# The sample's final state in a state-space layer: one set of fp32 products on row tiles, and a new order around scan 6

## The chip, the cores and the metric

The kernel runs on one core of a Trainium2 chip. The metric is the device time of one execution in microseconds (us), as a median over runs. TensorE is called PE (its weight loads PEld), VectorE DVE, ScalarE ACT, GpSimd POOL, and SyncE, which here issues most transfers, SP.

## What is computed

One step of a two-layer decoder trunk: a Mamba-2 (SSD) layer and a pooling layer, each with modulation, norm, gate and residual. Two inputs go through it: a prompt of 1024 new tokens, and a sample of 8 sequences with 8 tokens each and their stored states. The part that the change touches is the final state of the sample in the SSD layer. Each of 32 heads has a state of 64 x 128; four heads form a group, and eight groups are worked on one after another ("scan 0" to "scan 7").

```
def step(h, inp):            # per chunk; the sample has one chunk of 8 tokens
    s, d = inp
    return d[..., None, None] * h + s, h
chunk_states = einsum('bctgn,bctgr,bctgrp->bcgrpn', B, decay_end, xdt)
h_final, h_prev = lax.scan(step, h0, (chunk_states, chunk_decay))
```

For each of the 8 sequences the new state is thus the old one, decayed, plus a product of B and of the weighted x over that sequence's 8 tokens. The 64 sample tokens lie on partitions (twice, to fill 128), so this is a product whose sum runs over 8 of 64 rows.

## The kernel before

Everything in the SSD layer is paced by hand. `ssd_layer` runs eight calls of `scan`, and each has four steps p = 0 to 3 over 256 tokens. Between the pieces of a scan `units(fill, n)` puts in units of other work that PE can do at any time: 24 matmuls `mm` of the input projection of the next group (three matmuls for each of 8 slices of `hn`, split in high and low parts), and from scan 6's end the output product `op`. The table `PACE[g][p]` gives how many units go in at three places of a step. Each engine runs its instructions in the order of the code as a scheduler has merged them, so an instruction that waits holds up all behind it.

In step p, `scan_front(p + 1)` transposes x and B (`tr`, eight matmuls), `scan_state(p)` makes the chunk's states on PE (`S<-xd,Bt`) in the one PSUM bank with the tag "S", which DVE then adds to the running state (`h<-hd,S`), and `scan_y(p)` makes `y` in one of two banks of tag "y", which `scan_evac` empties on DVE (line 588, `xbc<-xbc,vec,y`). At steps p = 2 and 3 the sample is worked: `sample_front` makes Ms, the decays `ea`, the weighted x `xd` and the transposed B in `Bs`; `sample_prep` on p = 3 decays the old state h0 on POOL (line 682) and makes masked copies of x, one for each sequence (`st`, `xm`, ACT). The products themselves, `sample_state`, come during the next scan: half 0 (four sequences) at p = 0, behind y and am, and half 1 at p = 1. Each is four matmuls of 128 x 512 in fp32r, B split in a high and a low part, with one bank of tag "y" and the bank "S", an add on DVE (line 704) and a store on SP. In scan 7 both halves come at p = 0, the first with two "y" banks at its very start.

`ADA` lists the steps (g, p) at which a piece of the modulation vectors is computed. The first half of one is 16 matmuls (`am<-wr,scp`) in a "y" bank, copied by ACT as `mp` (line 266), the second half, after a unit, `am<-kc,mp`, which DVE reads as shf, scl or gat. `gate_norm` (`ms`) and `gate_scale` finish the scan before. The projection's weights come as `wr`, split by ACT and DVE into `wh` and `wl` (lines 152, 153); its result goes through a convolution of four steps: one on ACT, three on DVE (lines 356 to 361, `raw`, `xbc`). Around scan 6 and 7 the rows of gated y come back from memory (`row<-gyd`) and are combined in blocks on DVE (`b`, `bs`).

Of the kernel before, what the change touches and what calls it, by code (L numbers as in the profile page):

```python
# [7 lines left out]
F32 = mybir.dt.float32  # L8
F32R = mybir.dt.float32r
# [5 lines left out]
P = 128  # L15
# [20 lines left out]
         1: ((0, 0, 1), (1, 1, 1)), 4: ((0, 0, 1), (1, 0, 1)), 7: ((0, 0, 1),)}  # L36
LAST_USE = {4: 0, 7: 1}
LEAD = 3
PACE = (((1, 1, 1), (0, 1, 2), (0, 1, 2), (0, 1, 2)),) * 6 + (((1, 1, 1), (0, 1, 2), (0, 3, 5), (0, 1, 1)), ((1, 1, 1), (0, 1, 1), (0, 1, 1), (0, 1, 1)))
ADA = tuple((g, p) for g in range(7) for p in ((0, 1, 2) if g == 0 else (0, 2, 3) if g == 1 else (0, 2)))  # L40
NSLOT_A = 30
NSLOT_B = 7
NSLOT_E = 4
# [63 lines left out]
class Build:  # L107
# [298 lines left out]
    def proj_group(self, G):  # L406

        nc = self.nc
        for ii in range(4):
            w = self.stream_next()  # L410
            raw = self.proj_begin(G, ii)
            if (G["g"], ii) == (7, 3):

                ps = [self.mm_tile() for _ in CH]
                for k in range(8):
                    for c in range(3):
                        self.mm1(ps[c], w, k, self.hn[k], CH[c], k == 0, k == 7)
                    self.slots.free(*self.hn[k])
                    if k < 7:
                        yield  # L420
                for c in range(3):
                    self.proj_evict(G, ii, raw, ps[c], c)
                yield
                return
            for c, (a, n) in enumerate(CH):
                ps = self.mm_tile()
                self.mm3(ps, w, self.hn, CH[c])
                self.proj_evict(G, ii, raw, ps, c)
                yield
# [206 lines left out]
    def sample_front(self, s):  # L636

        nc, gp = self.nc, self.gs
        tok, col = slice(NP, TOK), 4 * s.g
        pt = self.pp.tile([P, 512], F32, tag="tr", bufs=2, name=self.name("tr"))  # L640
        for i, t in enumerate((s.xs[0], s.xs[1], s.B)):
            self.dup(pt[:, 128 * i:128 * i + 128], t[:, tok], self.ident)
        self.dup(pt[:, 384:448], s.B[:, tok], s.C[:, tok])
        A = gp.tile([P, 1024], F32, tag="M", bufs=2, name=self.name("Ms"))
        M, ea = (A[:, 256 * i:256 * i + 256].rearrange("p (r t) -> p r t", r=4) for i in range(2))
        xd = A[:, 512:1024].rearrange("p (i r q) -> p i r q", i=2, r=4)
        nc.vector.tensor_tensor(out=xd, in0=pt[:, 0:256].rearrange("p (r q) -> p r q", r=4).unsqueeze(1).to_broadcast([P, 2, 4, 64]),
                                in1=self.tks[:, :, col:col + 4].unsqueeze(3).to_broadcast([P, 2, 4, 64]), op=ALU.mult)
        Bt = gp.tile([P, 2, 128], F32R, tag="Bs", bufs=1, name=self.name("Bs"))
        nc.scalar.activation(Bt[:, 0], pt[:, 256:384], AF.Copy)  # L650
        nc.vector.tensor_tensor(out=Bt[:, 1], in0=pt[:, 256:384], in1=Bt[:, 0].bitcast(F32), op=ALU.subtract)
        cb = gp.tile([P, 256], F32, tag="cb", bufs=1, name=self.name("cb"))[:, :64]
        nc.vector.tensor_tensor(out=cb, in0=pt[:, 384:448], in1=self.kc[:, K_SMASK:K_SMASK + 64], op=ALU.mult)
        self.tab(nc.scalar.activation(ea, s.acs, AF.Exp))
        for r in range(4):
            nc.scalar.activation(M[:, r], s.acs[:, r], AF.Relu, bias=self.tka[2][:, col + r:col + r + 1], scale=-1.0)
        self.tab(nc.scalar.activation(M, M, AF.Exp, scale=-1.0))
        nc.vector.tensor_tensor(out=M, in0=M, in1=cb.unsqueeze(1).to_broadcast([P, 4, 64]), op=ALU.mult)
        s.sample = (M, ea, xd, Bt)
        self.slots.free(s.B, s.C)  # L660
# [12 lines left out]
        for q in range(2):  # L673
            self.scan_evac(s, q, py[:, q], slice(NP, TOK))

    def sample_prep(self, s):

        nc = self.nc
        _, ea, xd, _ = s.sample
        for i in range(2):  # L680
            h0 = s.hsl[i][:, :1024].rearrange("p (b r q) -> p b r q", b=4, r=4)
            nc.gpsimd.tensor_tensor(out=h0, in0=h0, in1=ea[:, :, 32 * i + 7:32 * i + 32:8].rearrange("p r b -> p b r").unsqueeze(3).to_broadcast([P, 4, 4, 64]), op=ALU.mult)
        xv = xd[:, 1].rearrange("p r q -> p (r q)")
        st = self.gs.tile([P, 256], F32R, tag="st", bufs=1, name=self.name("st"))
        nc.scalar.activation(st, xv, AF.Copy)
        nc.vector.tensor_tensor(out=st[64:], in0=xv[64:], in1=st[64:].bitcast(F32), op=ALU.subtract)
        s.xm = []
        for half in range(2):
            t = self.slots.get("xm", F32R)
            for i in range(4):  # L690
                b = 4 * half + i
                nc.scalar.activation(t[:, 256 * i:256 * i + 256], st.bitcast(F32), AF.Copy, scale=self.kc[:, K_SEQ + b:K_SEQ + b + 1])
            s.xm.append(t)

    def sample_state(self, s, half, tags=("y", "S")):

        Bt = s.sample[3]
        for i in range(2):
            S = self.pp.tile([P, 512], F32, tag=tags[i], bufs={"y": 2, "S": 1}[tags[i]], name=self.name("S"))
            xm = s.xm[half][:, 512 * i:512 * i + 512]  # L700
            self.te.matmul(S, Bt[:, 0], xm, start=True, stop=False)
            self.te.matmul(S, Bt[:, 1], xm, start=False, stop=True)
            d = s.hsl[half][:, 512 * i:512 * i + 512]
            self.nc.vector.tensor_tensor(out=d, in0=d, in1=S, op=ALU.add)
        self.nc.sync.dma_start(self.io["hsT"][s.g][:, 1024 * half:1024 * half + 1024], s.hsl[half][:, :1024])
        self.slots.free(s.hsl[half], s.xm[half])

    def gate_load(self, s):

# [739 lines left out]
    def fills(self):  # L1449

        for g in range(1, 7):
            yield from self.proj_fill(g)
        pr = self.proj_fill(7)
        yield from itertools.islice(pr, 9)
        self.op_begin(0)
        self.optags = ("mm",)
        self.rows = [None] * 16
        blk = self.block_steps(2, self.rows, False, 3, self.load_row)
        for j, _ in enumerate(pr):
            if j == 4:  # L1460
                for _ in range(2):
                    self.ow_fetch()
                self.ow_add()
            next(blk, None)
            yield
        self.ow_split()
        self.ow_fetch()
        self.ow_add()
        for _ in blk:
            pass  # L1470
        self.x = [None] * 8
        yield from self.out_fill()

# [5 lines left out]
    def ssd_layer(self):  # L1479

        self.pinned = True
        fill = self.fills()
        self.tc.keep_in_program_order(self.tab(self.nc.scalar.preload_act_table_set("natural_log_exp_and_others")))
        s = self.scans[0]
        self.scan_ac(s, 0)
        next(fill)
        self.scan_front(s, 0)
        self.scan_decay(s, 0)
        self.scan_ac(s, 1)
        for _ in range(LEAD - 1):  # L1490
            next(fill)
        for s in self.scans:
            self.scan(s, fill)
        self.units(fill, 2)
        self.gate_norm(s)
        self.sample_state(s, 0)
        self.units(fill, 2)
        self.sample_state(s, 1)
        self.gate_scale(s)
        self.pinned = False  # L1500
        self.fill = fill
# [11 lines left out]
    def scan(self, s, fill):  # L1513
# [2 lines left out]
        last, after = self.scans[g - 1] if g else None, self.scans[g + 1] if g < 7 else None  # L1516
        for p in range(4):
            a, b, c = PACE[g][p]
            if p == 0 and g == 7:
                self.sample_state(last, 0, ("y", "y"))  # L1520
            self.units(fill, a)
            if p < 3:
                self.scan_front(s, p + 1)
# [11 lines left out]
            if p == 2:  # L1535
                self.sample_front(s)
                self.sample_inter(s)
            if last and p == 1:
                self.gate_norm(last)
            ada = self.ada(g, p)  # L1540
            next(ada, None)
            if last and p == 0:
                self.sample_state(last, int(g == 7))
            if p == 2:
                self.gate_load(s)
                if g == 6:
# [1 line left out]
            elif p == 3:  # L1548
                if g < 6:
                    self.silu_burst(after.T)  # L1550
                self.sample_prep(s)
                if g == 7:
                    self.gate_rows(s)
            self.units(fill, min(c, 1))
            for _ in ada:
                pass
            if p == 1:
                if last and g < 7:
                    self.sample_state(last, 1)
                self.sample_load(s)  # L1560
            if last and p == 2:
                self.gate_scale(last)
            self.units(fill, c - min(c, 1))
            if p == 3 and after:
                if g == 6:
# [216 lines left out]
def _layout(inputs):  # L1782
# [59 lines left out]
    sc[[0, 128]] = 0  # L1842
    sc[256::8] = 0
    kc[:, K_SCAN:K_SCAN + 320] = sc
    kc[:, K_SEQ:K_SEQ + 8] = (np.arange(128)[:, None] % 64 // 8 == np.arange(8)[None, :])
    for gi, wd in enumerate(WINDOWS):
        for t in range(wd - 1):
            kc[:, K_CNT + 15 * gi + t] = wd / (t + 1.0)
# [34 lines left out]
```

## Time and profile before

| | before |
| --- | --- |
| median of 3 runs | 1656.43 us (1654.96 to 1656.57) |
| profiled execution | 1655.05 us |
| its span | 1653.1 us, mean granted clock 0.980 |
| PE busy | 1592.7 us, 96% |
| DVE, ACT, POOL busy | 76%, 50%, 29% |

The profile shows one execution. Busy time leaves out register, branch, semaphore and DMA-issuing instructions. An instruction's row gives its start, its duration, its line (a helper's, for matmuls L98), tile names out<-in, and in brackets the idle time ahead of it with what released it. The granted clock is 1.00 at 2.4 GHz and 0.50 at 1.2 GHz. The scans lie between about 283 and 900 us of the span.

### The profile page before, as it was taken

To read this page: it belongs to the slowest core of one execution; us is meant where nothing else is said; L and a number is where in the kernel's file an instruction comes from. 1 tells how busy PE (TensorE), PEld (TensorE's weight loads), DVE (VectorE), ACT (ScalarE), POOL (GpSimd) and SP (SyncE) were. 2 spreads that over 40 slices of the span, in tenths; PEclk is the share of its full clock that TensorE was granted. 3 is DMA by queue.
4 is the path that set the end of the run, shared out by engine and by line. 5 is a ranking of instruction groups with operands and counts; after the bars stand their busy time and mean duration, and the time that the engine had idled before them with its cause. 6 is when DMAs were issued, how large, how long until landed. Compare 5 with 4: busy or idle time off the path is not lost.

```text
span 1653.1 us, 30937 instructions
## 1 busy us (share of the span) xinstructions
PE 1592.7 (96%) x12335; PEld 1534.6 (93%) x12335; DVE 1248.2 (76%) x1984; ACT 831.8 (50%) x1485; POOL 475.4 (29%) x516
## 2 busy tenths in 40 slices
PE   8999999999999999998889999999999999999997
PEld 6899999999898989897878999999999999999997
DVE  6874476767777787767798878978889867577876
ACT  6653336666666757575754356633322234333364
POOL 0233441303121212213120122456666640000231
PEclk9999999999999999999889999999999999999999
DMA  8422226435454453637688883133323469566673
GB/s 342 160 98 95 87 73 226 145 111 172 156 167 150 144 194 113 212 117 266 175 287 313 219 196 124 57 110 113 112 90 110 135 204 380 153 169 179 162 155 117
DMA packets 103935, 272.31 MB, mean 165 GB/s; under 512 B 17744, under 2 KB 41712, under 8 KB 103792
## 3 DMA queue, kind: packets, MB, share of 16 engines
q1 hardware_dynamic: 95728, 244.91, 43.3%
q0 software_dynamic: 8064, 25.43, 8.8%
q8 instruction: 97, 1.59, 0.4%
q14 instruction: 46, 0.38, 0.1%
HBM read 208.99 MB, written 56.86 MB: 161 GB/s over the span
## 4 chain that ended last, share of the span: by engine, by line
PE 76%; DVE 10%; ACT 5%; issue 4%; DMA 4%; POOL 2%; SPq 0%; DVEq 0%; POOLq 0%; ACTq 0%
PE st L98 28%; PE mm L98 21%; PE op L98 14%; PE pl L98 3%; PE y L98 2%; DVE raw L358 2%; PE S L98 2%; PE am L98 1%; DMA x<-xT 1%; PE ms L98 1%; DVE M L562 1%; PE tr L98 1%; DVE xbc L359 1%; DMA rs<-rsd 1%; PE tr L101 1%
## 5 line engine op out<-in xcount | busy, mean ns | idle before, releaser
L98 PE MATMUL op<-b,w 128*128 128x272 f32 x2688 | 355.6, 294 | 15.9 <-ACT w L1141 5.4
L98 PEld LDWEIGHTS op<-b,w 128*128 128x128 f32 x2688 | 348.4, 193 | 22.4 <-DVE b L1082 7.0
L98 PE MATMUL st<-hh,w 128*128 128x272 f32 x1408 | 273.8, 289 | 0.0
L98 PE MATMUL mm<-hh,wh 128*128 128x364 f32 x720 | 247.9, 344 | 0.0
L98 PE MATMUL mm<-hl,wh 128*128 128x364 f32 x720 | 239.2, 332 | 0.0
L98 PE MATMUL mm<-hh,wl 128*128 128x364 f32 x720 | 239.0, 332 | 0.0
L98 PEld LDWEIGHTS st<-hh,w 128*128 128x128 f32 x1408 | 224.6, 189 | 0.3 <-issue 0.3
L98 PE MATMUL st<-t,w 128*128 128x272 f32 x1584 | 205.3, 288 | 0.0
L98 PE MATMUL st<-hl,w 128*128 128x272 f32 x704 | 203.5, 289 | 0.0
L98 PEld LDWEIGHTS st<-t,w 128*128 128x128 f32 x1584 | 201.0, 188 | 0.0
L98 PEld LDWEIGHTS mm<-hh,wh 128*128 128x128 f32 x720 | 137.8, 191 | 9.0 <-issue 6.7
L187 ACT ACTIVATE w<-wr 128x512 fp32r<-128x512 f32 x88 | 55.5, 631 | 176.0 <-PE st L98 145.4
L98 PEld LDWEIGHTS mm<-hl,wh 128*128 128x128 f32 x720 | 137.7, 191 | 1.3
L98 PEld LDWEIGHTS mm<-hh,wl 128*128 128x128 f32 x720 | 137.6, 191 | 0.0
L98 PEld LDWEIGHTS st<-hl,w 128*128 128x128 f32 x704 | 132.6, 188 | 0.0
L580 POOL TENSOR_TENSOR hd<-h,cd 128x256 f32<-128x256 f32 x56 | 64.3, 1148 | 135.5 <-DVE h L581 77.4
L1161 DVE SCALAR_TENSOR_TENSOR x<-op,gat,x 128x272 f32<-128x272 f32 (+1 forms) x160 | 72.9, 480 | 38.9 <-PE op L98 32.6
L1141 ACT ACTIVATE w<-wr 128x1024 fp32r<-128x1024 f32 x56 | 59.1, 1055 | 80.3 <-PE op L98 55.8
L363 POOL COPY ncv<-raw 128x3 f32<-128x3 f32 x32 | 8.9, 277 | 312.9 <-ACT raw L434 302.3
L558 ACT ACTIVATE M<-acb,tka 128x128 f32<-128x128 f32 x256 | 82.8, 389 | 25.3 <-PE y L98 15.8
L358 DVE SCALAR_TENSOR_TENSOR raw<-raw,vec,raw 128x1112 f32<-128x1112 f32 x64 | 89.0, 1390 | 6.1 <-ACT raw L356 5.8
L939 DVE TENSOR_TENSOR u<-st,u 128x272 f32<-128x272 f32 (+1 forms) x158 | 61.4, 409 | 39.7 <-PE st L98 37.7
(271 smaller groups left out, 3288.2 us busy)
## 6 DMA issues: line engine op xcount, KB each, us to landing
wr<-win SPq DMA_DIRECT2D x48, 512.0 KB, 3.5
acb<-acd SPq DMA_DIRECT2D x32, 512.0 KB, 5.8
wr<-pin SPq DMA_DIRECT2D x32, 512.0 KB, 3.6
wr<-wout SPq DMA_DIRECT2D x28, 512.0 KB, 6.4
wr<-pout SPq DMA_DIRECT2D x28, 512.0 KB, 4.7
row<-gyd SPq DMA_DIRECT2D x22, 544.0 KB, 7.0
wr<-wout POOLq DMA_DIRECT2D x20, 512.0 KB, 7.9
wr<-pout POOLq DMA_DIRECT2D x20, 512.0 KB, 5.9
```

Of the source, the lines that this page charges most:

```text
L98: return self.pin(self.build.nc.tensor.matmul(*a, **k))
L101: return self.pin(self.build.nc.tensor.transpose(*a, **k))
L187: self.nc.scalar.activation(hi, src, AF.Copy)
L358: nc.vector.scalar_tensor_tensor(out=acc[:, :n], in0=raw[:, k:k + n], scalar=w[k], in1=acc[:, :n], op0=ALU.mult, op1=ALU.add)
L359: nc.vector.scalar_tensor_tensor(out=dst[:, :NP], in0=raw[:, 3:3 + NP], scalar=w[3], in1=acc[:, :NP], op0=ALU.mult, op1=ALU.add)
L363: nc.gpsimd.tensor_copy(ncv[:, 0:1, :], raw[:, 1024:1027].unsqueeze(1))
L558: nc.scalar.activation(M[:, r, t], acb[:, r, t], AF.Relu, bias=self.tka[cc][:, col + r:col + r + 1], scale=-1.0)
L562: nc.vector.tensor_tensor(out=M, in0=M, in1=cb.unsqueeze(1).to_broadcast([P, 4, 256]), op=ALU.mult)
L580: nc.gpsimd.tensor_tensor(out=hd, in0=h, in1=cd[:, :, cc].unsqueeze(2).to_broadcast([P, 4, 64]), op=ALU.mult)
L939: nc.vector.tensor_tensor(out=out, in0=x, in1=y, op=ALU.add)
L1141: self.nc.scalar.activation(hi, r, AF.Copy)
L1161: ins = nc.vector.scalar_tensor_tensor(out=x[e][:, a:a + pn], in0=ps[:, :pn], scalar=g, in1=x[e][:, a:a + pn], op0=ALU.mult, op1=ALU.add)
```

## The change

The sample's state products are made at once. `sample_front` now keeps B in fp32, in two copies masked by ACT so that on each block of 32 partitions one sequence remains in each copy. `sample_state` runs eight fp32 matmuls of 32 rows by 256 columns, on four row tiles and into four banks (tags y, S, y, mm), each bank with two sequences. DVE adds the four banks in the order S[0], S[2], S[1], S[3], two for each half of the state. It stands once in each scan, at p = 0, behind the end of the ADA step there and so behind a unit. `st` and `xm` are gone. The decay (`sample_decay`) runs on DVE. `sample_load` moves to p = 0. For scan 7 `gate_norm` of the scan before comes at p = 0 and its `gate_scale` at p = 1, ahead of `sample_load`.

Around scan 6, the ADA step (6, 2) moves to (5, 3); three units instead of one follow in the third place of scan 6's step 3 and none in the second; the last projection tile yields once more before its eviction, and the blocks' steps that remain are made in the unit j = 7.

```diff
-PACE = ... (((1, 1, 1), (0, 1, 2), (0, 3, 5), (0, 1, 1)), ...
+PACE = ... (((1, 1, 1), (0, 1, 2), (0, 3, 5), (0, 0, 3)), ...
-ADA = ... (0, 2, 3) if g == 1 else (0, 2)
+ADA = ... (0, 2, 3) if g == 1 else (0, 2, 3) if g == 5 else (0,) if g == 6 else (0, 2)
...
-                    if k < 7:
-                        yield
+                    yield
...
-        Bt = gp.tile([P, 2, 128], F32R, tag="Bs", bufs=1, name=self.name("Bs"))
-        nc.scalar.activation(Bt[:, 0], pt[:, 256:384], AF.Copy)
-        nc.vector.tensor_tensor(out=Bt[:, 1], in0=pt[:, 256:384], in1=Bt[:, 0].bitcast(F32), op=ALU.subtract)
+        Bt = gp.tile([P, 2, 128], F32, tag="Bs", bufs=1, name=self.name("Bs"))
+        for i in range(2):
+            nc.scalar.activation(Bt[:, i], pt[:, 256:384], AF.Copy, scale=self.kc[:, K_SEQ + i:K_SEQ + i + 1])
...
-    def sample_prep(self, s):
+    def sample_decay(self, s):
...
-            nc.gpsimd.tensor_tensor(out=h0, in0=h0, in1=ea[...], op=ALU.mult)
+            self.nc.vector.tensor_tensor(out=h0, in0=h0, in1=ea[...], op=ALU.mult)
...
+    def sample_state(self, s):
+        _, _, xd, Bt = s.sample
         xv = xd[:, 1].rearrange("p r q -> p (r q)")
...
+        S = [self.pp.tile([P, 512], F32, tag=t, bufs=n, name=self.name("S")) for t, n in (("y", 2), ("S", 1), ("y", 2), ("mm", 3))]
+        for i in range(2):
+            for j in range(4):
+                rows = slice(32 * j, 32 * j + 32)
+                self.te.matmul(S[j][:, 256 * i:256 * i + 256], Bt[rows, i], xv[rows], start=True, stop=True, tile_position=(32 * j, 0))
         for half in range(2):
...
+            for i in range(2):
+                d = s.hsl[half][:, 512 * i:512 * i + 512]
+                self.nc.vector.tensor_tensor(out=d, in0=d, in1=S[half + 2 * i], op=ALU.add)
+            self.nc.sync.dma_start(self.io["hsT"][s.g][:, 1024 * half:1024 * half + 1024], s.hsl[half][:, :1024])
+        self.slots.free(*s.hsl)
...
-            next(blk, None)
-            yield
+            for _ in range(99 if j == 7 else 1):
+                next(blk, None)
+            if j < 8:
+                yield
...
-        self.sample_state(s, 0)
-        self.units(fill, 2)
-        self.sample_state(s, 1)
+        self.units(fill, 1)
+        self.sample_state(s)
...
-            if p == 0 and g == 7:
-                self.sample_state(last, 0, ("y", "y"))
...
-            if last and p == 1:
+            if last and p == int(g < 7):
                 self.gate_norm(last)
...
-            if last and p == 0:
-                self.sample_state(last, int(g == 7))
...
-            if p == 1:
-                if last and g < 7:
-                    self.sample_state(last, 1)
-                self.sample_load(s)
-            if last and p == 2:
+            if p == 0:
+                if last:
+                    self.sample_state(last)
+                if g < 7:
+                    self.sample_load(s)
+            if last and p == (2 if g < 7 else 1):
                 self.gate_scale(last)
+                if g == 7:
+                    self.sample_load(s)
```

How the order on the engines changes is shown at three places. First PE in scan 6 (scans 1 to 5 alike), from the end of the ADA step at p = 0 on. Here mp is ACT's copy, Ms the tile whose second half holds the weighted x, kc the identity, xbc the group's x and B. Before:

```order
L98 MATMUL am_8106<-kc,mp_8115 128x9 x2
L101 MATMUL tr_8166<-kc,xbc_7550 128x128
L101 MATMUL tr_8166<-kc,xbc_7771 128x128
...
L101 MATMUL tr_8167<-kc,xbc_7134 128x128 x2
L98 MATMUL tr_8167<-xbc_7351,xbc_7134 128x128 x2
L98 MATMUL S_8178<-xd_8031,Bt_8032 128x256 x2
```

The same place with the change:

```order
L98 MATMUL am_8047<-kc,mp_8056 128x9 x2
L98 MATMUL S_8098<-Ms_7605,Bs_7607 128x256
L98 MATMUL S_8099<-Ms_7605,Bs_7607 128x256
L98 MATMUL S_8100<-Ms_7605,Bs_7607 128x256
L98 MATMUL S_8101<-Ms_7605,Bs_7607 128x256
...
L101 MATMUL tr_8124<-kc,xbc_7485 128x128
L101 MATMUL tr_8124<-kc,xbc_7706 128x128
...
L101 MATMUL tr_8125<-kc,xbc_7069 128x128 x2
L98 MATMUL tr_8125<-xbc_7277,xbc_7069 128x128 x2
L98 MATMUL S_8136<-xd_7972,Bt_7973 128x256 x2
```

The state products (twice the four) now stand between the end of am and the transposes; S_8099 holds the bank "S", which S_8136 takes next.

Second, DVE at the same place: gat reads am, raw and xbc are the convolution, h the running states, hd their decayed copies. Before:

```order
L300 TENSOR_SCALAR gat_263<-am_8106,adab_256 128x9 x2
L546 TENSOR_TENSOR xd_8176<-tr_8166,tkx 128x2x256 x2
L153 TENSOR_TENSOR wl_8215<-wr_8212,wh_8214 128x1024
L358 SCALAR_TENSOR_TENSOR raw_8154<-raw_7992,vec,raw_8154 128x1112
L581 TENSOR_TENSOR h_8181<-hd_8182,S_8178 128x256
```

With the change:

```order
L300 TENSOR_SCALAR gat_263<-am_8047,adab_256 128x9 x2
L153 TENSOR_TENSOR wl_8173<-wr_8170,wh_8172 128x1024
L694 TENSOR_TENSOR h_125_7308<-h_125_7308,S_8098 128x512
L358 SCALAR_TENSOR_TENSOR raw_8086<-raw_7933,vec,raw_8086 128x1112
L694 TENSOR_TENSOR h_125_7308<-h_125_7308,S_8100 128x512
L358 SCALAR_TENSOR_TENSOR raw_8086<-raw_7933,vec,raw_8086 128x1112
L694 TENSOR_TENSOR h_126_7310<-h_126_7310,S_8099 128x512
L359 SCALAR_TENSOR_TENSOR xbc_8085<-raw_7933,vec,raw_8086 128x1024
L361 SCALAR_TENSOR_TENSOR xbc_8085<-raw_7933,vec,raw_8086 128x64
L694 TENSOR_TENSOR h_126_7310<-h_126_7310,S_8101 128x512
L580 TENSOR_TENSOR h_8139<-hd_8140,S_8136 128x256
```

The add that reads S_8099 is the third of the four and stands behind wl and two steps of the convolution; xd of the next step went behind them all.

Third, DVE in scan 7 (w is a weight block of the output product, b a block of rows). Before:

```order
L704 TENSOR_TENSOR h_147_8317<-h_147_8317,S_8805 128x512
L704 TENSOR_TENSOR h_147_8317<-h_147_8317,S_8809 128x512
L1142 TENSOR_TENSOR w_8817<-wr_8634,w_8816 128x1024
L577 COPY h_8871<-S_8868 128x256
L546 TENSOR_TENSOR xd_8866<-tr_8856,tkx 128x2x256 x2
```

With the change:

```order
L694 TENSOR_TENSOR h_134_8116<-h_134_8116,S_8938 128x512
L694 TENSOR_TENSOR h_134_8116<-h_134_8116,S_8940 128x512
L1072 TENSOR_TENSOR b_8934<-bs_8600,b_8934 128x544
L694 TENSOR_TENSOR h_135_8118<-h_135_8118,S_8939 128x512
L694 TENSOR_TENSOR h_135_8118<-h_135_8118,S_8941 128x512
L545 TENSOR_TENSOR xd_8966<-tr_8956,tkx 128x2x256
```

Here too the four adds stand together, with a block of rows between the second and the third, and the next step's xd behind them.

## Rows read from the trace of the kernel before

**Rows 1.** The page's busy times: us, share of the span, instructions.

```profile
PE 1592.7 (96%) x12335; PEld 1534.6 (93%) x12335; DVE 1248.2 (76%) x1984; ACT 831.8 (50%) x1485; POOL 475.4 (29%) x516
```

**Rows 2.** PE's waits, 360 to 760 us: waiter, releaser: us in total, times, longest.

```profile
PE S L98 <- DVE xbc L588: 10.4, 6, 2.1
PE am L98 <- issue: 1.7, 1, 1.7
```

**Rows 3.** Stretches am to S<-xd,Bt: us, busy PE, PEld, DVE, ACT, POOL, clock, DMA.

```profile
361.77:372.74 10.97, 9.11 (x60) 8.10 (x59) 6.12 (x10) 6.29 (x15) 0.04 (x1) 0.84 0.73 230
...
735.74:745.16 9.42, 7.57 (x60) 6.76 (x59) 5.93 (x10) 6.29 (x15) 0.04 (x1) 1.00 0.74 242
sum 60.37, PE 49.96 PEld 44.93 DVE 35.33 ACT 37.63 POOL 0.28; mean PE 8.33 PEld 7.49 DVE 5.89 ACT 6.27 POOL 0.05
```

**Rows 4.** Timeline of PE, scan 6: start us, us, instruction, wait ahead and releaser.

```profile
735.74 1.07 PE L98 MATMUL am<-wr,scp 128*32 128x256 f32 x16
738.66 1.17 PE L98 MATMUL S<-xm,Bs 128*128 128x512 f32 x4 [1.85 <-DVE xbc L588]
739.67 0.33 PE L98 MATMUL mm<-hh,wh 128*128 128x360 f32 x1
...
743.66 0.51 PE L98 MATMUL am<-kc,mp 128*128 128x9 f32 x4
...
745.16 1.03 PE L98 MATMUL S<-xd,Bt 128*128 128x256 f32 x4
```

**Rows 5.** Timeline of DVE, the same place.

```profile
744.28 0.36 DVE L300 TENSOR_SCALAR gat<-am,adab 128x9 f32<-128x9 f32 x2 [3.44 <-PE am L98]
...
745.90 1.22 DVE L153 TENSOR_TENSOR wl<-wr,wh 128x1024 fp32r<-128x1024 f32 x1
747.04 1.37 DVE L358 SCALAR_TENSOR_TENSOR raw<-raw,vec,raw 128x1112 f32<-128x1112 f32 x1
```

**Rows 6.** Timeline of ACT, the same place.

```profile
743.70 1.06 ACT L152 ACTIVATE wh<-wr 128x1024 fp32r<-128x1024 f32 x1 [2.20 <-PE mm L98]
...
745.21 1.32 ACT L356 ACTIVATE raw<-raw,vec 128x1112 f32<-128x1112 f32 x1
```

**Rows 7.** The S adds and the decay: ns min/median/max, first and last start.

```profile
L704 DVE TENSOR_TENSOR h<-h,S x32: 673/680/690, 365.8 to 886.5; 128x512 f32<-128x512 f32 x32
...
L682 POOL TENSOR_TENSOR h<-h,Ms x16: 1927/2156/2907, 324.6 to 859.6; 128x1024 f32<-128x1024 f32 x16
```

**Rows 8.** Stretches at the lower clock: us, PE busy, clock, DMA share, GB/s.

```profile
665.24:668.65 3.41, 3.41 (x14) 0.50 0.90 303
781.29:788.12 6.83, 6.25 (x22) 0.50 1.00 312
798.36:805.18 6.82, 5.43 (x52) 0.50 1.00 272
829.07:835.90 6.83, 5.66 (x21) 0.50 0.83 254
```

**Rows 9.** PE's waits, 762 to 890 us.

```profile
PE am L98 <- ACT mp L266: 5.3, 1, 5.3
PE S L98 <- DVE h L704: 5.2, 1, 5.2
PE op L98 <- DVE b L1082: 4.0, 3, 1.4
```

**Rows 10.** Timelines of DVE and POOL beside each other, scan 6.

```profile
776.90 2.95 DVE L562 TENSOR_TENSOR M<-M,cb 128x1024 f32<-128x1024 f32 x1
...
774.47 4.31 POOL L682 TENSOR_TENSOR h<-h,Ms 128x1024 f32<-128x1024 f32 x2
```

**Rows 11.** Timeline of DVE, scan 7.

```profile
821.96 1.23 DVE L562 TENSOR_TENSOR M<-M,cb 128x1024 f32<-128x1024 f32 x1 [0.59 <-ACT M L559]
826.46 0.50 DVE L1161 SCALAR_TENSOR_TENSOR x<-op,gat,x 128x272 f32<-128x272 f32 x1 [3.28 <-DMA x<-xT]
...
829.50 0.68 DVE L704 TENSOR_TENSOR h<-h,S 128x512 f32<-128x512 f32 x1
```

More of the change, by code (lines that the diff above doesn't have):

```diff
@@ L38 @@
 LEAD = 3
-PACE = (((1, 1, 1), (0, 1, 2), (0, 1, 2), (0, 1, 2)),) * 6 + (((1, 1, 1), (0, 1, 2), (0, 3, 5), (0, 1, 1)), ((1, 1, 1), (0, 1, 1), (0, 1, 1), (0, 1, 1)))
-ADA = tuple((g, p) for g in range(7) for p in ((0, 1, 2) if g == 0 else (0, 2, 3) if g == 1 else (0, 2)))
+PACE = (((1, 1, 1), (0, 1, 2), (0, 1, 2), (0, 1, 2)),) * 6 + (((1, 1, 1), (0, 1, 2), (0, 3, 5), (0, 0, 3)), ((1, 1, 1), (0, 1, 1), (0, 1, 1), (0, 1, 1)))
+ADA = tuple((g, p) for g in range(7) for p in ((0, 1, 2) if g == 0 else (0, 2, 3) if g == 1 else (0, 2, 3) if g == 5 else (0,) if g == 6 else (0, 2)))
 NSLOT_A = 30
@@ L674, in sample_y @@
             self.scan_evac(s, q, py[:, q], slice(NP, TOK))
-    def sample_prep(self, s):
-        nc = self.nc
-        _, ea, xd, _ = s.sample
+    def sample_decay(self, s):
+        ea = s.sample[1]
         for i in range(2):
             h0 = s.hsl[i][:, :1024].rearrange("p (b r q) -> p b r q", b=4, r=4)
-            nc.gpsimd.tensor_tensor(out=h0, in0=h0, in1=ea[:, :, 32 * i + 7:32 * i + 32:8].rearrange("p r b -> p b r").unsqueeze(3).to_broadcast([P, 4, 4, 64]), op=ALU.mult)
+            self.nc.vector.tensor_tensor(out=h0, in0=h0, in1=ea[:, :, 32 * i + 7:32 * i + 32:8].rearrange("p r b -> p b r").unsqueeze(3).to_broadcast([P, 4, 4, 64]), op=ALU.mult)
@@ L683, in sample_prep @@
+    def sample_state(self, s):
+        _, _, xd, Bt = s.sample
         xv = xd[:, 1].rearrange("p r q -> p (r q)")
[L684 to L687, printed above, removed]
-        for half in range(2):
[L689 to L706, printed above, removed]
+        S = [self.pp.tile([P, 512], F32, tag=t, bufs=n, name=self.name("S")) for t, n in (("y", 2), ("S", 1), ("y", 2), ("mm", 3))]
@@ L1468, in fills @@
         self.ow_add()
-        for _ in blk:
-            pass
         self.x = [None] * 8
@@ L1550, in scan @@
                     self.silu_burst(after.T)
-                self.sample_prep(s)
+                self.sample_decay(s)
                 if g == 7:
@@ L1844, in _layout @@
     kc[:, K_SCAN:K_SCAN + 320] = sc
-    kc[:, K_SEQ:K_SEQ + 8] = (np.arange(128)[:, None] % 64 // 8 == np.arange(8)[None, :])
+    for j in range(4):
+        for i in range(2):
+            b = 32 * j + 16 * (j // 2) + 8 * i
+            kc[b:b + 8, K_SEQ + i] = 1.0
     for gi, wd in enumerate(WINDOWS):
```

## The prediction

> **What bounds the kernel now.** I read the busy line first: PE works 1592.7 of 1653.1 us [rows 1], so only what PE executes or waits for can move the time. Then PE's waits between 360 and 760 us, the middle of the scans: two groups alone, the state products S waiting six times for the DVE line that empties bank y (10.4 us together, 2.1 the longest), and one 1.7 us wait of am [rows 2]. So in scans 1 to 6 the rest of p=0 to p=3 runs without a gap, and what the change does there is read from one stretch: from the start of am<-wr,scp to the S<-xd,Bt of p=1. Over the six scans it takes 60.37 us; in three of them the granted clock is 0.84, as in the first row, in the other three 1.00, as in the second [rows 3]. Scan 6 shows its inside [rows 4]: am 1.07, wait 1.85, S 1.01, a unit of 24 matmuls 3.99, and from am<-kc,mp to S<-xd,Bt 1.50 us (743.66 to 745.16) with the transposes in it and no wait.
>
> **What the change makes of it, scans 1 to 6.** Now S comes after the unit and am<-kc,mp: the unit covers the 1.85 us in which DVE empties y, and that wait goes. The second S pair, at p=1, goes too: 1.01 us by the pair shown [rows 4]. So before costs 60.37 + 6 x 1.01 = 66.4 us.
>
> After, PE's order is am<-kc,mp, eight S, eight transposes, S<-xd,Bt. The last one needs the bank "S", which S[1] now holds; the fence on DVE shows that the add which reads it is the third one, behind wl and two conv steps. I count it from t0, the start of am<-kc,mp, with scan 6's own rows. ACT: wh ends at t0 + 1.10 (743.70 + 1.06), two evictions follow, the conv's first step ends at 746.53, t0 + 2.87 [rows 6]. DVE: the two gat end at t0 + 0.98; wl (1.22) waits for wh and ends at t0 + 2.32; then add 0.68, conv 1.37, add 0.68, conv 1.37, add 0.68 [rows 5, 7]: t0 + 7.1. Neighbours overlap by 0.08 (745.90 + 1.22 is 747.12, and the conv step starts at 747.04), which for four steps takes this to t0 + 6.8. The conv step's own condition, t0 + 2.87, is met on time. So S<-xd,Bt starts at t0 + 6.8 instead of t0 + 1.5. The stretch becomes 1.07 + 3.99 + 6.8 = 11.86, six times 71.2: **4.8 us more** than 66.4.
>
> The products themselves don't enter that sum. Two 128x256 fp32 products are four records, 1.03 us with their tail [rows 4]; eight of them take 4.1 us one after another, about 1.0 if four tiles run at once. With 1.1 us of transposes both end before t0 + 6.8. PE then idles 1.2 (serial) to 4.3 us. If they ran one after another the adds would come later too, by about 1.2 us a scan; I take the parallel end, since the tiles write four different banks, and keep +7 us for the other.
>
> One rule of the Trainium skill speaks against this change (TensorEngine Tiling (Array Packing), PSUM Bottleneck): tiling speeds up TensorE but not the emptying of PSUM, which may become what limits. The rows bear it out: each add of 128x512 takes 0.68 us before and after. By the page's up to fourfold speedup alone (Theoretical Speedup), an estimate, the products would fall from 2.0 us a scan to a part of it, and the time with them; that result is the third rival.
>
> **The clock.** The granted clock falls to 0.50, the 1.2 GHz level, after waits of PE. The stretch took 10.97 us in scan 1, where it fell, and 9.42 in scan 6, where it didn't, with about the same wait: one drop costs 1.5 us. It lasted 3.41 us there (the like of it in scan 5 is shown); three drops between 780 and 836 us lasted 6.8 us, with 5.4 to 6.3 us of PE work in them, so 2.7 to 3.1 lost [rows 3, 8]. After waits of about 1.85 us the clock fell in some scans only; after the 5.3 and 5.2 us waits [rows 9] it fell both times. The new wait, some 4 us, is nearer to these, but I take the short drop, since a full-speed unit stands ahead of it: 6 x 1.5 = **9.0 us**, bounds 0 and 6 x 2.9 = 17.
>
> **Other edits in scans 1 to 6.** Decay from POOL (2.16 us each [rows 7]) to DVE: two multiplications of the size of M, 1.23 us each when nothing disturbs them [rows 11], about 2.5 us a scan. DVE has room at p=3: PE has no wait for it there [rows 2], and POOL's disturbance goes (below). The eight xm copies on ACT, st and the subtraction for Bs leave; ACT and DVE don't bind there. sample_load moves from p=1 to p=0, two 512 KB loads earlier on SP, behind the stores of the previous state; h0 is used at p=2, so this costs nothing. If DVE's cover fails, y(p) would wait by some 1.3 us a scan. ADA step (6,2) moves to (5,3), a p=3 step, where scan 1's shows a 1.7 us wait of am [rows 2]; with the matmuls (am 1.07, am<-kc,mp 0.36) that is **3.1 us**, to be set against what scan 6 saves.
>
> **Scan 6 and 7.** Here before wastes much: PE waits 5.32 us for mp, 5.16 for the bank S, 4.0 for b [rows 9]. The first: ACT makes mp behind a burst of silu, and DVE is slow beside POOL's decay (M takes 2.95 us against 1.23, while POOL's two decays run 4.31) [rows 10, 11]. The second: DVE waits 3.28 us for x<-xT, with the S add at 829.50 behind it [rows 11]. A half-speed stretch follows each of these three, with PE busy 6.25, 5.43 and 5.66 us in it: half of that, 8.7 us, is lost too [rows 8]. So 14.5 + 8.7 = 23.2 us stand to be won. The am steps are gone from scan 6's p=2, DVE is free of POOL there, three more op units stand at p=3, S of scan 6 no longer sits ahead of the x<-xT wait. What comes in, stepped through by hand with before's durations: y at p=3 waits about 3 us for h behind six subtractions of b on DVE; the single S<-xd,Bt of scan 7 waits about 3.5 for the third add; y and the S bank 3.5 elsewhere; and half-speed stretches behind two of them (2 x 2.8). 23.2 - 3 - 3.5 - 3.5 - 5.6 - 3.1 (the moved ADA step) = **4.5 us won**, bounds 0 and about 13, since by the same steps DVE comes out some 90% busy there and passes little on.
>
> **Sum.** 4.8 + 9.0 - 4.5 = 9.3 us more, 1664.4. The sum is made against the profiled execution, 1655.05 us (1653.1 of span); the median of the runs shown is 1656.43, 1.4 more, and the same sum gives 1665.7 there. I say 1664.
>
> **The rivals.**
> *The reorder around scan 6 gives more than the six waits cost.* If all three waits and their stretches go, and only the ADA step and few new waits come (under 3 us), scan 6 and 7 win some 17 to 20, net 1655 + 13.8 - 20 = 1649: faster. It decides from a gain of 14 us. For it: those waits are the largest of the profile. Against: DVE, which releases most of the waits there, has little room in the new order. Chance 0.18.
> *No clock drop behind the new waits.* 4.8 - 4.5: 1655 to 1656, within 0.2%. For it: waits of 1.85 us passed without one in some scans [rows 3]. Against: neither wait of over 5 us did [rows 9]. Chance 0.18.
> *The adds are not late.* Then the stretch is 1.07 + 3.99 + 0.36 + 1.0 + 1.1 = 7.5, six times 45: 21 us less than 66.4, and with 4.5 of scan 6 and 7 about 1630. DVE's fixed order speaks against it. Chance 0.04.
> *The change doesn't do what it says:* the tiles run one after another, 7 us more: 1671. Chance 0.06.
> *Long drops, 6.8 us, behind each wait:* 17 in place of 9.0, 1672. For it: all drops behind the long waits around scan 6 were long [rows 8, 9]. Chance 0.10.
>
> **How the numbers follow.** My own case keeps 0.44. A measurement of this kernel can tell about 0.2%, 3.3 us, from no change. Slower: 0.44 + 0.06 + 0.10 = 0.60. Same: the second rival and the edge of the first, 0.20. Faster: the first without its edge and the third, 0.20. The range goes from 1650, which cuts off the third rival and half of the first, to 1677, the long drops with the late adds of serial tiles in some scans.
>
> **What would show it.** In the changed trace: S<-xd,Bt of p=1 waits 3 to 4.3 us on the S add in scans 1 to 6, six times, with PEclk near 0.8 in the stretch and half-speed behind each; the stretch lasts some 12 to 13 us; "S <- xbc" waits are gone; eight S records of about 0.4 us overlapping. am's 5.3 us wait is gone in scan 6, and one of about 1.7 us stands at scan 5's p=3. A stretch under 9 us, or a clock of 1.00 in it, or scans 6 and 7 shorter by over 14 us would prove me wrong.

## The result, and the profile after

| | before | changed |
| --- | --- | --- |
| median, the runs shown | 1655.7 us (4 runs) | 1666.62 us (4 runs) |
| ratio, 95% interval | | 1.0069 (1.0052 to 1.0087) |
| span of the profiled execution | 1653.1 us | 1663.9 us |

The change makes the kernel 0.7% slower, 11 us. PE's waits between 360 and 760 us (columns as in [rows 2]) show why:

```profile
PE S L98 <- DVE h L694: 17.4, 5, 3.5
PE am L98 <- issue: 3.6, 2, 1.8
```

The wait for the line that empties y is gone. In its place S waits for the adds of the sample's state (L694), 3.5 us each; the same happens once more in scan 6 and once in scan 7. The am wait is there twice, as the ADA step now stands in scan 5 too. The stretches from am<-wr,scp to S<-xd,Bt, as in [rows 3]:

```profile
361.82:373.80 11.98, 8.46 (x72) 7.08 (x71) 8.77 (x14) 9.30 (x23) 2.82 (x5) 0.93 0.69 219
...
519.13:531.12 11.99, 8.53 (x73) 7.08 (x71) 8.75 (x13) 10.48 (x25) 2.82 (x5) 1.00 0.64 217
...
749.99:762.05 12.06, 8.55 (x73) 7.16 (x71) 8.28 (x12) 10.48 (x25) 4.08 (x7) 0.97 0.80 196
sum 72.05, PE 51.14 PEld 42.63 DVE 51.56 ACT 60.55 POOL 18.17; mean PE 8.52 PEld 7.11 DVE 8.59 ACT 10.09 POOL 3.03
```

They answer to 60.37 us, plus the second pairs, before. All six take 12.0 us: the wait doesn't vary, since it is a count of instructions on DVE. Scan 6 from inside, PE as in [rows 4] and then DVE as in [rows 5]:

```profile
749.99 1.07 PE L98 MATMUL am<-wr,scp 128*32 128x256 f32 x16
...
755.09 0.51 PE L98 MATMUL am<-kc,mp 128*128 128x9 f32 x4
755.53 1.75 PE L98 MATMUL S<-Ms,Bs 32*128 32x256 f32 x16
757.21 0.87 PE L101 MATMUL tr<-kc,xbc 128*128 128x128 f32 x6
757.92 0.61 PE L98 MATMUL tr<-xbc,xbc 128*128 128x128 f32 x4
762.05 0.76 PE L98 MATMUL S<-xd,Bt 128*128 128x256 f32 x1 [3.51 <-DVE h L694]
```

```profile
755.64 0.36 DVE L300 TENSOR_SCALAR gat<-am,adab 128x9 f32<-128x9 f32 x2 [0.82 <-PE am L98]
756.22 1.22 DVE L153 TENSOR_TENSOR wl<-wr,wh 128x1024 fp32r<-128x1024 f32 x1 [0.21 <-ACT wh L152]
757.36 0.68 DVE L694 TENSOR_TENSOR h<-h,S 128x512 f32<-128x512 f32 x1
758.04 1.38 DVE L358 SCALAR_TENSOR_TENSOR raw<-raw,vec,raw 128x1112 f32<-128x1112 f32 x1
759.34 0.68 DVE L694 TENSOR_TENSOR h<-h,S 128x512 f32<-128x512 f32 x1
759.93 1.37 DVE L358 SCALAR_TENSOR_TENSOR raw<-raw,vec,raw 128x1112 f32<-128x1112 f32 x1
761.22 0.68 DVE L694 TENSOR_TENSOR h<-h,S 128x512 f32<-128x512 f32 x1
```

From 755.09 (am<-kc,mp): wl, the first add, a conv step, the second add, a conv step, and at 761.22 the third, which ends 6.81 us after it. PE has been ready since 758.5 and starts S<-xd,Bt at 762.05, 6.96 us after. In four of the six scans of this execution the lower clock begins in the wait, 0.6 to 1.8 us before S<-xd,Bt, and lasts beyond it (columns as in [rows 8]):

```profile
372.23:379.06 6.83, 5.26 (x16) 0.50 0.52 161
454.15:457.56 3.41, 2.81 (x8) 0.50 0.57 192
679.43:686.26 6.83, 5.06 (x15) 0.50 0.63 229
761.35:768.18 6.83, 6.13 (x19) 0.50 1.03 325
```

In seven profiled executions of the experiments below that keep these waits it came in or right behind five or six of the six. From S<-xd,Bt to y takes 5.03 us in scans 3 and 4, where no drop follows, 6.4 us with a drop of 3.4 us, and 7.4 to 7.9 with one of 6.8: a drop costs 1.4 to 2.9 us. Over the six scans that is 9.0 us here, and 9.2 to 13.4 in the seven others.

The span in three stages, cut at the am<-wr,scp of scan 1, at that of scan 6, and where the pool layer's products st<-hh,w begin; columns as in [rows 3]. Before:

```profile
361.77:735.74 373.97, 363.70 (x2902) 340.73 (x2900) 277.31 (x384) 245.16 (x501) 81.39 (x135) 0.99 0.49 158
735.74:1075.94 340.20, 309.26 (x2419) 295.01 (x2418) 282.20 (x482) 189.60 (x335) 76.02 (x86) 0.94 0.69 205
1075.94:1653.10 577.16, 565.81 (x4290) 564.16 (x4288) 447.01 (x706) 205.46 (x313) 219.10 (x189) 0.99 0.51 157
```

The changed kernel:

```profile
361.82:749.99 388.17, 367.15 (x2962) 340.83 (x2960) 274.67 (x386) 230.58 (x463) 59.90 (x125) 0.98 0.47 155
749.99:1087.65 337.66, 306.92 (x2423) 291.24 (x2421) 278.23 (x479) 185.36 (x328) 69.07 (x83) 0.94 0.69 202
1087.65:1663.90 576.25, 564.56 (x4290) 563.01 (x4288) 446.15 (x706) 205.78 (x313) 217.64 (x189) 0.99 0.51 157
```

So 14.2 us are lost from scan 1 to 6, 2.5 won from there to the pool layer, and 0.9 in the rest, 10.8 in all. The first stage adds up: the stretches of scans 1 to 5 are 9.0 us longer, the second pairs are gone (5 x 1.01), the drops behind the waits cost 6.2 (7.5 + 6.4 + 7.4 against 3 x 5.03), the ADA step 3.2 (1.8 of wait, 1.4 of products): 13.4 of 14.2. Around scans 6 and 7, from 762 to 900 us, these are PE's four largest groups of waits, to be set beside [rows 9]:

```profile
PE S L98 <- DVE h L694: 7.0, 2, 3.5
PE tr L101 <- ACT xbc L394: 3.3, 1, 3.3
PE S L98 <- DVE xbc L587: 2.8, 1, 2.8
PE y L98 <- DVE h L580: 2.1, 2, 1.8
...
```

The am wait of 5.3 us is gone; new are the waits of tr, of S for xbc, and most of that of y (0.8 us before). The 4.0 us of op on b have left this window, but not the kernel: from 897.6 us on op waits for b at its end.

```profile
901.32 2.14 PE L98 MATMUL op<-b,w 128*128 128x272 f32 x7 [3.73 <-DVE b L1072]
```

Over the whole second stage op waits 5.3 us for b before and 5.1 after. PE's idle time there, the stage less busy PE in the rows above, is 30.9 us before and 30.7 after, with scan 6's new wait in it: waits changed their place more than they went.

### The profile page after: what moved, and what is told of

The parts are those of the page before. It is cut to its first block, busy times and chain, and to the rows that moved or that the text cites. A ratio compares the mean times of both kernels' runs of the same rounds, so it can differ in the third digit from the quotient of the medians.

```text
span 1663.9 us, 31028 instructions
## 1 busy us (share of the span) xinstructions
PE 1593.2 (96%) x12399; PEld 1530.0 (92%) x12399; DVE 1240.6 (75%) x1984; ACT 807.1 (49%) x1421; POOL 440.9 (27%) x500
## 4 chain that ended last, share of the span: by engine, by line
PE 81%; DVE 8%; DMA 4%; issue 3%; ACT 3%; POOL 1%; SPq 0%; DVEq 0%; POOLq 0%; ACTq 0%
PE mm L98 28%; PE st L98 28%; PE op L98 11%; PE y L98 3%; PE pl L98 3%; PE S L98 2%; PE am L98 2%; DMA wr<-wout 1%; DVE w L1132 1%; PE tr L98 1%; PE tr L101 1%; DVE raw L358 1%; PE ms L98 1%; DVE b L1072 1%; DMA wr<-pout 1%
## 5 line engine op out<-in xcount | busy, mean ns | idle before, releaser
L579 POOL TENSOR_TENSOR hd<-h,cd 128x256 f32<-128x256 f32 x56 | 55.3, 987 | 160.4 <-DVE h L580 70.1
L189 POOL TENSOR_TENSOR w<-wr,w 128x512 fp32r<-128x512 f32 x44 | 79.2, 1800 | 37.6 <-ACT w L187 37.4
```

Of the source, the lines that this page charges most:

```text
L189: eng.tensor_tensor(out=lo, in0=src, in1=hi.bitcast(F32), op=ALU.subtract)
L579: nc.gpsimd.tensor_tensor(out=hd, in0=h, in1=cd[:, :, cc].unsqueeze(2).to_broadcast([P, 4, 64]), op=ALU.mult)
```

## Experiments

My theory: the wait is there because S[1] holds the one bank "S" and its add comes third; the drops are a second term; the reorder around scan 6 gives a few us back. The rival on the wait: DVE as a whole is late there, and the bank only shows it. All times below are compared with runs of the kernel before on the same chip.

**1. Another bank for S[1].**

```diff
-for t, n in (("y", 2), ("S", 1), ("y", 2), ("mm", 3))
+for t, n in (("S", 1), ("y", 2), ("y", 2), ("mm", 3))
```

> The change, but S[0], whose add comes first on VectorE, takes the bank S, and S[1] takes a y bank. Theory (the scan's own product waits for the third add only because S[1] sits in its bank): the start of S<-xd,Bt moves from 6.95 us after am<-kc,mp to about 3.4 (behind the transposes), the wait of 3.5 us and the clock drops behind it go: 6 x 3.4 = 20 us, some 8 to 10 us of drops, about 3 in scan 7, so some 1634 us (1630 to 1642). Rival (VectorE's work as a whole is late, whichever bank comes first): the wait reappears at y of p=1, which needs h behind all four adds, at about the same size, and the time stays at 1660 to 1667.

Measured: 1647.89 us, ratio 0.9938 (0.9916 to 0.9961): faster than before, 19 us better than the change by the medians, but not the 1634 expected. A stretch, the waits between 360 and 760 us, and PE in scan 1:

```profile
659.31:667.62 8.31, 8.31 (x73) 7.08 (x72) 4.94 (x9) 6.83 (x16) 2.82 (x5) 1.00 0.57 189
```

```profile
PE tr L98 <- DVE xd L545: 7.9, 5, 3.3
...
```

```profile
396.88 1.26 PE L98 MATMUL tr<-kc,xbc 128*64 128x128 f32 x12 [3.32 <-DVE xd L545]
```

The stretch is 8.3 us at a clock of 1.00, without any wait: the bank was the cause of that wait. But part of it comes back at p = 2, where the sample's transposes wait for xd, which on DVE stands behind the adds, 0.8 to 3.3 us each in scans 1 to 5. Two drops of 3.4 us fall in this stage too, one from 397.20, right behind the wait shown, and one from 714.70, behind a 1.8 us wait of am in scan 5. The rival holds for that part, at another place than it said.

**2. The adds in another order.**

```diff
-        for half in range(2):
+        for half in (1, 0):
```

> The change, with the halves added the other way round; on VectorE the add of S[1] then comes second, behind wl and one convolution step. Theory: S<-xd,Bt starts about 5.0 us after am<-kc,mp, the wait is about 1.6 us in place of 3.5, 6 x 1.9 = 11 us less, and some clock drops go (waits of that size were followed by one in three of five scans before): 1648 to 1655 us. Rival (VectorE as a whole): no change, 1664 to 1668.

Measured: 1644.15 us, ratio 0.9922 (0.9903 to 0.9942). By the code S[1] and S[3] are now added first; in the order that the scheduler gave DVE the adds are those of S[0], S[1], S[3] and S[2]. The first two in scan 6 (a conv step stands between them), PE's waits, then a stretch and the first two stages:

```profile
741.41 0.68 DVE L694 TENSOR_TENSOR h<-h,S 128x512 f32<-128x512 f32 x1
...
743.39 0.68 DVE L694 TENSOR_TENSOR h<-h,S 128x512 f32<-128x512 f32 x1
```

```profile
PE S L98 <- DVE h L694: 9.0, 6, 1.5
...
```

```profile
657.68:667.68 10.00, 8.47 (x72) 7.05 (x70) 6.70 (x11) 8.53 (x21) 2.82 (x5) 1.00 0.62 197
361.79:734.04 372.25, 361.33 (x2962) 335.62 (x2960) 272.50 (x386) 228.96 (x463) 60.06 (x125) 1.00 0.50 162
734.04:1067.30 333.26, 303.63 (x2423) 286.31 (x2421) 277.11 (x479) 185.06 (x328) 74.09 (x83) 0.96 0.70 204
```

The add of S[1] comes second and ends at 744.07, S<-xd,Bt starts at 744.13, and the wait is 1.5 us, as expected. The stretch is 10.0 us, 2.0 less. No drop followed any of the six waits: the clock is 1.00 over the whole first stage. That is why the time lies below the 1648 to 1655 expected: 15.9 us are won in that stage (388.17 to 372.25), 10 of them by the waits, the others by the drops. One line of order, with the same work, turns a loss of 0.7% into a gain of 0.8%.

**3. The wait filled with work.**

```diff
+            if last and after and p == 1:
+                ps = self.mm_tile()
+                for _ in range(20):
+                    self.te.matmul(ps[:, :128], self.ones, self.ones, start=True, stop=True)
             self.scan_state(s, p)
```

> The change, with 20 fp32 products of 128x128 of a constant, which nobody reads, on PE between the transposes and S<-xd,Bt of p=1 in scans 1 to 6: some 3.4 us of work in a wait of 3.5 us. The third add still sets the start of S<-xd,Bt. Theory (the clock drops behind the waits are a term of their own, about 9 us): the stretches stay at 12.0 us, no drop follows them, 1655 to 1660 us. Rival (the drops cost nothing that a later wait would not have taken): 1665 to 1669.

Measured: 1658.72 us, ratio 1.0024 (1.0008 to 1.0041). PE in scan 1, then a stretch and the first two stages:

```profile
369.93 4.63 PE L98 MATMUL mm<-ones 128*128 128x128 f32 x40
374.39 1.03 PE L98 MATMUL S<-xd,Bt 128*128 128x256 f32 x4
```

```profile
668.90:681.67 12.77, 12.77 (x113) 11.55 (x111) 9.58 (x13) 10.91 (x26) 2.82 (x5) 1.00 0.59 207
361.62:749.64 388.02, 384.09 (x3163) 359.14 (x3161) 275.63 (x386) 231.00 (x463) 65.06 (x125) 1.00 0.47 155
749.64:1080.18 330.54, 305.77 (x2463) 290.50 (x2461) 278.80 (x479) 185.59 (x328) 70.37 (x83) 0.96 0.70 206
```

PE does useless work for 4.5 us, more than I had reckoned, and a stretch is 12.77 us, 0.8 longer than with the wait. Yet the kernel is 8 us faster than the change by the medians, and no drop follows any of the six stretches in this execution. In the first stage the two profiled executions are equal (388.02 against 388.17): the five stretches are 4.1 us longer, am in scan 5 loses 1.6 us to a drop that the change's execution hasn't (3.4 us from 727.30, behind am's own 1.8 us wait), and the 6.2 us of drops behind the waits are gone. The remainder lies in the second stage, 330.54 against 337.66: 2.1 us of it in scan 6 (0.8 longer, 2.9 of drop gone), the others behind it, where waits moved as well (in scan 7 S waits 0.9 us for the adds, not 3.5). That there is a clock term is shown. The medians would put it at 12 to 13 us (8, and 0.8 for each of six stretches), but how much of this is the waits' that moved isn't shown; its size also differs from execution to execution with the number and length of the drops.

**4. The products tile by tile.**

```diff
-        for i in range(2):
-            for j in range(4):
+        for j in range(4):
+            for i in range(2):
```

> The change, with the eight products issued tile by tile (both of a tile one after the other) in place of one round over the four tiles after another. Theory (four tiles run at once, and the products are hidden in the wait anyway): the products take longer than the 1.7 us of the change, up to 2.7, which is what sixteen records take one after another, but the stretch stays at 12.0 to 12.1 us and the time at 1664 to 1669. Rival (the products are on the path): each 0.1 us of them shows six times.

Measured: 1665.31 us, one run. PE in scan 6:

```profile
756.40 1.75 PE L98 MATMUL S<-Ms,Bs 32*128 32x256 f32 x16
...
762.92 0.77 PE L98 MATMUL S<-xd,Bt 128*128 128x256 f32 x1 [3.51 <-DVE h L694]
```

The products take the same 1.7 us and the wait is the same 3.5. I had expected them to become slower; in this one run the issue order of the tiles makes no difference, so it doesn't test what their time is worth. That they aren't on the path is read from the rows of the change: PE waits 3.5 us behind them, and none of DVE's adds in scan 6 waits for them.

**5. The order around scan 6 as before** (PACE, ADA, the projection's yields, the blocks' steps), run twice; the second time beside the change itself.

```diff
-PACE = ... (0, 3, 5), (0, 0, 3)), ...
+PACE = ... (0, 3, 5), (0, 1, 1)), ...
-ADA = ... else (0, 2, 3) if g == 5 else (0,) if g == 6 else (0, 2))
+ADA = ... else (0, 2))
...
-                    yield
+                    if k < 7:
+                        yield
...
-            for _ in range(99 if j == 7 else 1):
-                next(blk, None)
-            if j < 8:
-                yield
+            next(blk, None)
+            yield
...
+        for _ in blk:
+            pass
```

> The change with PACE, ADA, the last projection tile's yields and the blocks' steps as before, so only the state products, the decay and their places are new. Theory (the reorder around scan 6 is worth 4.5 us and more): 1670 to 1676 us, with am's wait for mp back in scan 6. Rival (the reorder gives nothing, since the step moved to scan 5 costs 5 us there): 1660 to 1666.

> The order around scan 6 as before, in a second measurement. Theory A: 1660 to 1663 us, with an interval that lies below that of the change. Theory B: within 2 us of the change.

> The change itself, beside the next two on the same chip: its reorder around scan 6 had been taken for a gain of 4.5 us, and undoing it gave a ratio of 1.0039 where the change has 1.0069. Theory A (the reorder costs some 5 us while the long waits stand) and theory B (it is worth nothing that can be told) both give 1664 to 1668 here.

Measured: 1661.47 us, ratio 1.0039 (1.0025 to 1.0054), and 1662.30, 1.0044 (1.0029 to 1.0058); the change beside the second 1667.94, 1.0079 (1.0060 to 1.0097). The intervals of the pair just don't meet: the reorder costs some 5.6 us (5 by the first run). The first theory fell, its rival and theory A of the second run hold. PE's waits from 762 to 900 us, first without the reorder (second run), then the change beside it:

```profile
PE S L98 <- DVE h L695: 7.5, 2, 4.0
...
PE y L98 <- DVE h L577: 2.4, 1, 2.4
...
PE am L98 <- ACT mp L266: 1.0, 1, 1.0
...
PE tr L101 <- ACT xbc L394: 0.4, 1, 0.4
```

```profile
PE S L98 <- DVE h L694: 6.5, 2, 3.5
PE tr L101 <- DVE xd L545: 3.7, 1, 3.7
PE S L98 <- DVE xbc L587: 2.8, 1, 2.8
...
```

Without the reorder am stands in scan 6, and it waits 1.0 us for mp, not 5.3. So the long wait of before had gone through the other parts of the change (which of them wasn't tried), and moving the ADA step bought little. The reordered kernel waits with the first transposes of scan 7 (for xd here; in the execution above for ACT's silu of xbc, which starts at 815.50 behind a table load and a split of w) and longer with S for xbc. But these waits don't make up the loss: in this window all of PE's waits come to 20.6 us without the reorder and 19.1 with it. The whole second stage, in the same order:

```profile
750.33:1082.15 331.82, 303.98 (x2443) 288.68 (x2441) 279.68 (x482) 187.42 (x329) 69.35 (x83) 0.96 0.71 208
753.75:1091.32 337.57, 304.63 (x2423) 287.59 (x2421) 278.10 (x479) 185.21 (x328) 68.98 (x83) 0.96 0.69 202
```

In these two executions the stage is 5.7 us longer with the reorder, and PE idles 5.1 us more in it (32.9 against 27.8), most of it behind 900 us, where op waits 6.0 us for b with the reorder and 0.4 without. But in the profiled execution of the first run, the slowest of that run, the stage takes 336.9 us without the reorder too. So the loss is shown by the medians, twice, and which waits make it up isn't shown.

**6. Parts of the reorder.** Only the ADA step back, and only PACE back (the ADA lines and the PACE lines of the diff above).

> The change with only the ADA step back at scan 6, p=2. Theory A, in its likeliest form (the step's wait and products at scan 5 are the loss, and in scan 6 the step would be nearly free): 1660 to 1663 us. Theory B: within 2 us of the change.

> The change with only the units' numbers at scan 6, p=3 as before (one unit ahead of y, one behind it, and one fewer before scan 7). Theory (the place of the units is what makes the reorder lose 5.6 us: y of p=3 and the first transposes of scan 7 come while VectorE and ScalarE are late): 1660 to 1664 us. Rival (it is the yields and the blocks' steps, or the three parts only together): within 2 us of 1667.

Measured: 1668.33 us, ratio 1.0073 (1.0046 to 1.0100), and 1666.24, ratio 1.0082 (1.0057 to 1.0107). By the medians neither part alone brings the 5.6 us back, and both theories miss; the lower ends of the intervals, about 1662 us both, still reach into their ranges. The yields and the blocks' steps alone weren't run, so whether they are the cause, or only all parts together, stays open.

**7. The adds in the other order, with the old order around scan 6, whole and in part.**

> The halves added the other way round, and the order around scan 6 as before. Theory (the two effects add up: 22 us won by the one, 5 by the other): 1637 to 1642 us. Rival (the reorder costs only where the long waits stand): 1643 to 1648.

> The halves added the other way round, and of the reorder only the ADA step back at scan 6, p=2. Theory (the step's wait at scan 5, 1.7 us, and its 1.4 us of products are what the reorder loses, and am no longer waits long for mp in scan 6 since GpSimd is out of the way): 1638 to 1642 us. Rival (am's wait for mp of 5.3 us comes back with its clock drop): 1644 to 1650.

Measured: 1641.71 us, ratio 0.9921 (0.9902 to 0.9940), and 1643.12, ratio 0.9929 (0.9912 to 0.9947). The first number lies in its theory's range, the second between theory and rival. But beside experiment 2's 0.9922 both ratios are the same, where the theory wanted 5 us less. The two effects don't add up: where the long waits are short, the reorder neither loses nor wins anything that can be told (each interval reaches 3 us to either side). All three are faster than both kernels, by 0.7 to 0.8% than before.

**8. The decay back on GpSimd.**

```diff
-            self.nc.vector.tensor_tensor(out=h0, ...
+            self.nc.gpsimd.tensor_tensor(out=h0, ...
```

> The change with the decay left on GpSimd. Theory (the decay is beside the path on either engine in scans 0 to 5, and only disturbs VectorE in 6 and 7): 1665 to 1671 us. Rival (two multiplications more on VectorE are part of the loss): 1655 to 1663.

Measured: 1667.69 us, ratio 1.0075 (1.0056 to 1.0094), the same as the change. The decay is beside the path on either engine.

## Why the prediction was right, point by point

- *The new wait.* Right, to 0.2 us: third add, start at t0 + 6.96 where 6.8 was forecast, stretch 12.0 against 11.86. Experiments 1 and 2 move it by bank and by order as the count says (8.3, 10.0 and 12.0 us for the first, second and third add), which rules out the rival in which the adds aren't late, and most of the one in which DVE as a whole sets it.
- *The clock.* Right in kind; 9.0 us were forecast from six short drops. In the profiled execution four drops followed, three of them long, and cost 9.0 us: the same sum from other parts, which is luck. In seven other executions five or six followed and cost 9.2 to 13.4, so the term was rather too small. A short drop cost 1.4 to 1.6 us (1.5 forecast), a long one 2.3 to 2.9, as forecast. The reason for taking the short one, a full-speed unit ahead, didn't hold: that unit stands ahead of all six waits. The rival "no drop" fell; "long drops behind each wait" is half true. One sign of being wrong came: the clock is 1.00 in the stretches of scans 3 and 4, and 0.93 to 0.98 in the others, not near 0.8. The drops begin at the end of the stretch at the earliest and lie mostly behind it, so that sign was sought at the wrong place.
- *The ADA step at scan 5.* Right: 1.8 us of wait and 1.4 of products, 3.2 against 3.1.
- *Scans 6 and 7.* Here the size was off and, within it, a reason. 4.5 us net was forecast, which is 7.6 won without the ADA step. Measured from scan 6's am on: 2.5 won, though scan 6's own stretch and drop lose there: 2.6 longer, 1.0 less for the second pair, 2.9 of drop, so 4.5. Without that 7.0 were won against 7.6, but by other terms, so this agreement is luck in part. am's wait of 5.3 us went, and S waits 3.5 in scan 7, both as forecast. But op's wait for b, counted as 4.0 won, only moved (5.3 in the whole stage before, 5.1 after), and the 3.3 of tr had no term. The reorder, to which I gave part of the gain, is a loss of some 5.6 us (experiment 5), so the gain comes from the other parts. I had put am's 5.3 us wait down to its place behind the silu; experiment 5 shows it down to 1.0 us at the same place.
- *Nothing from the decay, the copies and the loads.* The decay is shown (experiment 8). Of the copies and loads no wait shows in scans 1 to 5; they weren't tried alone.
- *The tiles.* Eight products took 1.7 us, between the ends 1.0 and 4.1; they are hidden, as said: PE waits 3.5 us behind them. The serial end was reckoned too high, since it counts the tail of 0.35 us four times: four records take 0.68 us without it, so sixteen 2.7.
- *The sum.* 9.3 us forecast, 10.8 in the profiled execution. Up to scan 6's am 14.6 was forecast (five times 2.3 and the ADA step) against 14.2; scan 6's own stretch and drop lost 4.5 against 2.3, scans 6 and 7 behind it won 7.0 against 7.6, and 0.9 in the rest had no term: -0.4 + 2.2 + 0.6 - 0.9 = 1.5.

## What to carry to other kernels

When work moves behind another piece of the same engine, look at which of its buffers the next piece needs, and count the instructions that stand ahead of its release on the reading engine: here the order of four adds decided between 1.007 and 0.992 of the time. A wait of 3.5 us cost more than itself, since the clock mostly fell behind it; one of 1.5 us, at the same place, cost only its length. A reorder tuned around old waits should be tried again alone once these waits have moved.

## What the runs showed of the hardware

- The same place in the program, with waits of 1.5 us: no drop of the clock in scans 1 to 6 of three executions (18 waits). With waits of 3.5 us: four to six drops in six, of 3.4 or 6.8 us (eight executions). With the waits filled with products: none behind them in one execution.
- am's 1.8 us wait in scan 5's step 3 was followed by a drop of 3.4 us in two of eight executions (experiments 1 and 3).
- The products on row tiles overlap but don't run at full overlap: sixteen records of 32 rows by 256 columns took 1.68 us, where four of 128 by 256 take 0.68 us one after another (2.7 for sixteen). In scan 6 part of it is the wait of the third tile for its bank: its first record starts 0.6 us behind the first tile's, and the last twelve records take 1.1 us.
